# A two-layer hybrid trunk: gated retention output turned by DMA, the gate's projection finished by token halves, weights requested in another order

## The chip, the cores and the metric

One core of a Trainium2 chip runs the whole kernel. The metric is the device time of one execution in microseconds (us). A core has five engines with a queue of instructions each: TensorE (PE; PEld is its weight load), VectorE (DVE), ScalarE (ACT), GpSimd (POOL) and SyncE (SP). An engine works through its queue in order, and an instruction that waits holds all that stand behind it. SyncE issues nearly all transfers (DMA).

## The reference, cut to what matters

Two layers run over x of 256 tokens by 1024. In each, one projection makes eight groups of 512 columns, RQ RK RV RZ for the retention heads and MQ MK MV MZ for the attention heads; the two gated outputs go side by side through w_out; then a gated embedding is added. The part that the change touches is the retention output and its gate:

```python
h = rms_norm(x, norm_g[i])
proj = h @ w_in[i]
rq, rk, rv, rz, mq, mk, mv, mz = jnp.split(proj, cuts, axis=-1)
r_out = retention(rotary(heads(rq, RET_HEADS), pos), rotary(heads(rk, RET_HEADS), pos),
                  heads(rv, RET_HEADS), ret_norm_g[i])
r_out = jax.nn.silu(rz.astype(f32)) * r_out
...
y = jnp.concatenate([r_out, m_out], axis=-1).astype(x.dtype) @ w_out[i]
x = x + y
gate = jax.nn.sigmoid((rms_norm(x) @ w_ple_gate[i]).astype(f32))
e = rms_norm(p[i] @ w_ple[i], ple_norm_g[i]).astype(f32)
x = x + (gate * e).astype(x.dtype)
```

All is float32. The retention output is normalised per head and multiplied by the gain ret_norm_g.

## The kernel before

The tokens stand in two halves of 128 (m = 0, 1). Every large product is done with three TensorE matmuls (`mm3`, L136): weights and activations are split into a high part (wh, ah: a cast to fp32r) and a low part (wl, al: the rest), and hi x hi, hi x lo and lo x hi are summed in PSUM.

A block of weights is 512 rows by 512 columns, 1 MB; each group of 512 columns needs two, half 0 and half 1 of the 1024 rows. The list `jobs` holds their loads in the order of use. `fetch` (L102) issues loads from SyncE until the wanted one is there and more than AHEAD = 3 loaded ones are unused. `load_w` (L123) fetches a block and splits it in two pieces, with a cast on ScalarE (L131) and a subtraction on VectorE (L132) each. Four blocks fit in the buffers wst, six pieces in wh and six in wl.

The order per layer is MQ, MK, MV, MZ, RQ, RK, RV, RZ, then w_out, then the gate of the embedding. TensorE's and SyncE's queues keep the order of the program. For ScalarE, VectorE and GpSimd a scheduler sets the order when the kernel is built. Work that belongs between the matmuls is put there by `later(n, f)`: it runs f after n ticks, and a tick comes after every six matmuls of `project`.

`project` (L379) makes the groups MQ, MK, MV, RV and RZ with tokens on the partitions: for each block, four k by two m, k outermost; m is outermost only in the second block of MQ in layer 1 (L387). `project_turned` (L437) makes RQ and RK with the head's columns on the partitions, and for each head `rope` (L479) reads the accumulator: ScalarE copies one half of it (L486), VectorE adds the other (L487), which frees it. There are four accumulators, so head 2 of RK needs the one of head 2 of RQ. `moba_scores` (L518), its `turn` and `moba_out` (L561, whose matmuls have lines L566 and L567) are the attention's steps that lie between these.

q and k of the attention are turned from tokens to columns by DMA: `qk_norm` (L416) makes the rows, `halves` (L396) splits each float into two 16-bit halves on ScalarE (L399), and 6 + m ticks later `to_heads` (L402) issues a 16-bit DMA transpose from SyncE (L407) and puts the halves together again with two VectorE copies (L412). SyncE also writes the row scales out (`spread`) and reads them back over all partitions (`gather`, hrow), and loads the constants cst, which rope reads.

The retention output is turned on TensorE. `ret_out` (L590) leaves the normalised rows in RO. `gate` (L500) makes silu's factor of RZ from a tanh (L504) and L505. `ret_gate` (L611) multiplies both (L613); 4 + m ticks later its `turn` does four 128x128 transposes on TensorE into PSUM (L242), and `evac_parts` (L244) multiplies by the gain (L250), casts the high part (L253) and subtracts for the low part (L254). The result yT[m], blocks 0 to 3, is read by the last part of w_out: first both column halves n of the attention's rows of w_out (half 1, 48 matmuls), then those of the retention's rows (half 0) for m = 0 and for m = 1. After that come the embedding's product and the gate's.

## Time and profile before

| what | us |
|---|---|
| median of 3 runs | 320.6 (320.49 to 322.58) |
| profiled execution, its own time | 321.39 |
| span of the profiled execution | 319.5 |
| TensorE busy in the span | 311.8 |
| VectorE busy | 240.0 |
| ScalarE busy | 197.5 |
| GpSimd busy | 27.4 |

The profile is of one execution. Its span runs from the first to the last instruction of the core; the execution's own time also has what lies around it. Times in the trace count from the start of the span. Matmuls are pipelined: a row's duration is longer than the distance to the next one. An idle time in brackets is that of the engine just before the instruction, with what ended it.

### The profile page before, as it was taken

The page shows a single profiled execution, that of the slowest core. Times are in us where ns is not written, and L with a number is a line of the kernel's source. Part 1 is how long each engine was busy: PE and PEld are TensorE (multiplying, and loading weights), DVE is VectorE, ACT ScalarE, POOL GpSimd, SP SyncE. Part 2 cuts the span into 40 slices and gives each one's busy share as a digit, 9 for nine tenths or more (in the row PEclk, how much of TensorE's full clock was granted, in tenths as well). Part 3 has the DMA queues.
Part 4 walks back from the last instruction along what each step waited for, and adds up shares of the span by engine and source line. Part 5 has one row for each costly group of instructions (what it writes and reads, how often), then busy time and mean ns, then how long its engine had stood idle before and what let it go on. Part 6 is the DMA issues. An engine that isn't in the chain of part 4 may idle for free.

```text
span 319.5 us, 4520 instructions
## 1 busy us (share of the span) xinstructions
PE 311.8 (98%) x1625; PEld 264.8 (83%) x1625; DVE 240.0 (75%) x436; ACT 197.5 (62%) x378; POOL 27.4 (9%) x45
## 2 busy tenths in 40 slices
PE   8999999979999999999999999999999999999994
PEld 4888899868888888888888888998888888888884
DVE  4797856979967985958798877586799669859632
ACT  5878836986943544836485987559769424438411
POOL 4014200000001100011001521000000011000000
PEclk9999999999999999999999999999999999999999
DMA  7996999742673365000997169973345533610001
GB/s 272 416 401 210 284 291 416 263 147 118 228 267 132 131 242 188 0 2 4 373 409 255 78 151 247 389 286 131 131 144 201 184 133 131 220 44 2 33 33 68
DMA packets 19126, 61.13 MB, mean 191 GB/s; under 512 B 9628, under 2 KB 10656, under 8 KB 12960
## 3 DMA queue, kind: packets, MB, share of 16 engines
q1 hardware_dynamic: 19096, 60.85, 54.5%
q8 instruction: 13, 0.21, 0.3%
q14 instruction: 9, 0.07, 0.1%
q10 hardware_dynamic: 8, 0.00, 0.0%
HBM read 57.69 MB, written 1.06 MB: 184 GB/s over the span
## 4 chain that ended last, share of the span: by engine, by line
PE 74%; DMA 9%; ACT 8%; DVE 4%; issue 2%; SPq 1%; ACTq 0%
PE acc L139 17%; PE acc L141 17%; PE acc L140 17%; DMA wst<-in_w_in 6%; PE acc L449 6%; ACT wh L131 3%; PE acc L450 3%; PE mix L242 2%; PE mix L557 2%; DMA E<-in_rest 2%; DVE wl L132 2%; DMA w<-u 2%; PE acc L472 1%; PE acc L470 1%; PE acc L468 1%
## 5 line engine op out<-in xcount | busy, mean ns | idle before, releaser
L132 DVE TENSOR_TENSOR wl<-wst,wh 128x1024 fp32r<-128x1024 f32 x96 | 115.8, 1221 | 26.8 <-ACT wh L131 26.6
L131 ACT CAST wh<-wst 128x1024 fp32r<-128x1024 f32 x96 | 98.5, 1051 | 59.5 <-PE acc L141 30.4
L139 PE MATMUL acc<-wh,a 128*128 128x512 f32 (+1 forms) x296 | 116.4, 393 | 0.0
L140 PE MATMUL acc<-wl,a 128*128 128x512 f32 (+1 forms) x296 | 113.8, 385 | 0.1
L141 PE MATMUL acc<-wh,a 128*128 128x512 f32 (+1 forms) x296 | 113.8, 384 | 0.0
L141 PEld LDWEIGHTS acc<-wh,a 128*128 128x128 f32 x296 | 55.6, 188 | 11.2
L139 PEld LDWEIGHTS acc<-wh,a 128*128 128x128 f32 x296 | 55.8, 189 | 10.7 <-ACT wh L229 0.6
L140 PEld LDWEIGHTS acc<-wl,a 128*128 128x128 f32 x296 | 55.8, 189 | 10.6 <-DVE wl L236 0.6
L449 PE MATMUL acc<-a,wh 128*128 128x512 f32 x128 | 46.6, 406 | 2.0 <-DVE tmp L487 2.0
L450 PE MATMUL acc<-a,wl 128*128 128x256 f32 x128 | 35.8, 280 | 0.0
L449 PEld LDWEIGHTS acc<-a,wh 128*128 128x128 f32 x128 | 24.1, 188 | 7.6 <-issue 1.9
L450 PEld LDWEIGHTS acc<-a,wl 128*128 128x128 f32 x128 | 24.2, 189 | 0.1
L468 PE MATMUL acc<-a,wh 128*128 128x256 f32 x64 | 18.6, 291 | 0.0
L472 PE MATMUL acc<-a,wl 128*128 128x256 f32 x64 | 18.1, 283 | 0.0
L470 PE MATMUL acc<-a,wh 128*128 128x256 f32 x64 | 18.1, 283 | 0.0
L712 ACT ACTIVATE tmp<-acc,hr 128x512 f32<-128x512 f32 (+1 forms) x9 | 5.8, 640 | 19.4 <-PE acc L141 17.7
L152 POOL TENSOR_TENSOR ro<-rs_t,neghalf 128x4 f32<-128x4 f32 x4 | 4.0, 1007 | 142.7 <-DVE rs_t L151 142.7
L713 DVE SCALAR_TENSOR_TENSOR tmp<-tmp,E 128x512 f32<-128x512 f32 (+1 forms) x9 | 5.7, 631 | 13.7 <-ACT tmp L712 13.7
L412 DVE COPY T<-w 128x512 uint16<-128x512 uint16 x16 | 6.4, 459 | 9.0 <-DMA w<-u 9.0
L468 PEld LDWEIGHTS acc<-a,wh 128*128 128x128 f32 x64 | 12.3, 192 | 0.1
L470 PEld LDWEIGHTS acc<-a,wh 128*128 128x128 f32 x64 | 12.3, 192 | 0.1
L472 PEld LDWEIGHTS acc<-a,wl 128*128 128x128 f32 x64 | 12.2, 191 | 0.0
(119 smaller groups left out, 376.4 us busy)
## 6 DMA issues: line engine op xcount, KB each, us to landing
wst<-in_w_in SPq DMA_DIRECT2D x30, 1024.0 KB, 8.4
wst<-in_w_out SPq DMA_DIRECT2D x8, 1024.0 KB, 4.7
wst<-in_w_gate SPq DMA_DIRECT2D x8, 1024.0 KB, 4.8
wst<-in_w_ple SPq DMA_DIRECT2D x2, 1024.0 KB, 4.7
wst<-in_rest SPq DMA_DIRECT2D x4, 384.0 KB, 6.6
E<-in_rest SPq DMA_DIRECT2D x3, 384.0 KB, 4.0
x_t<-in_x SPq DMA_DIRECT2D x2, 512.0 KB
gb<-in_ple_g SPq DMA_DIRECT2D x2, 512.0 KB, 4.4
```

The lines of the kernel that those rows point to most:

```text
L131: nc.scalar.copy(hi, s)
L132: nc.vector.tensor_tensor(lo, s, hi.bitcast(F32), op=ALU.subtract)
L139: nc.tensor.matmul(ps, ah[:, k], wh[:, kk], start=start, stop=False)
L140: nc.tensor.matmul(ps, ah[:, k], wl[:, kk], start=False, stop=False)
L141: nc.tensor.matmul(ps, al[:, k], wh[:, kk], start=False, stop=stop)
L242: nc.tensor.transpose(ps[:, j * P:(j + 1) * P], src[:, b * P:(b + 1) * P], ident)
L412: nc.vector.tensor_copy(raw[:, t], w[:, t])
L449: nc.tensor.matmul(ps[h], wh[:, k % 2, sl], aB[:, kk], start=kk == 0, stop=False)
L450: nc.tensor.matmul(ps[h][:, 0], wl[:, k % 2, sl], aB[:, kk, 0], start=False, stop=end)
L468: nc.tensor.matmul(o, wh[:, k % 2, sl], aB[:, kk, 0], start=kk == 0 and h % 2 == 0, stop=False, skip_group_check=True)
L470: nc.tensor.matmul(o, wh[:, k % 2, sl], aB[:, kk, 1], start=False, stop=False, skip_group_check=True)
L472: nc.tensor.matmul(o, wl[:, k % 2, sl], aB[:, kk, 0], start=False, stop=end, skip_group_check=True)
```

## The change

The four parts of the change:

- `ret_gate` no longer turns its product on TensorE. It splits it into 16-bit halves (`halves`, moved out and shared), and 1 + 2m ticks later `parts_by_dma` issues a DMA transpose from SyncE, puts the halves together with two VectorE copies into a tile in SBUF and gives that to `evac_parts`.
- The second block of RZ is done for m = 0 first and then for m = 1.
- `fetch` no longer loads ahead. `ahead` does so at the end of `load_w` and `load_first`, after the block's split has been put into the program, and when the block counts as used; so one block more is requested there than before.
- The constants are requested after the second block of RQ instead of after the first, the transposes of q and k come at tick 7 + m instead of 6 + m, and `spread` at 8 instead of 9.

```diff
     def fetch(key):
 
-        while key not in got or len(got) - len(used) <= AHEAD:
-            if not jobs:
-                break
-            k, fn = jobs.pop(0)
-            r = fn()
-            if k is not None:
-                got[k] = r
+        while key not in got:
+            load_next()
         used.add(key)
         return got[key]
+
+    def load_next():
+        k, fn = jobs.pop(0)
+        r = fn()
+        if k is not None:
+            got[k] = r
+
+    def ahead():
+
+        while jobs and len(got) - len(used) <= AHEAD:
+            load_next()
...
             parts.append((hi, lo))
+        ahead()
         return parts
...
+    def turned_by_dma(u, raw):
+
+
+        w = tok_p.tile([P, 2, 4, P], U16, name="w16", bufs=2)
+        nc.sync.dma_start(w.rearrange("p t h k -> p (t h) k"), u.rearrange("p t n -> p (t n)"),
+                          transpose=True)
+        for t in range(2):
+            nc.vector.tensor_copy(raw[:, t], w[:, t])
+
+    def parts_by_dma(a, k0, u, gains=None):
+
+        with tc.high_priority(offset=PRIO):
+            f = tmp_p.tile([P, GW], F32, name="tmp")
+            turned_by_dma(u, f.bitcast(U16).rearrange("p (j k t) -> p t j k", j=4, t=2))
+            evac_parts(a, k0, f, 4, gains)
...
-                if l == 0 and g == RQ and not half:
+                if l == 0 and g == RQ and half:
                     job(None, lambda: nc.sync.dma_start(cst, consts))
...
-                if half and l and g == MQ:
+                if half and (g == RZ or l and g == MQ):
                     rows.sort(key=lambda r: r[1])
...
-                later(6 + m, lambda m=m, u=u: to_heads(g, m, u, qkg[:, l:l + 1] if g == MQ else None))
+                later(7 + m, lambda m=m, u=u: to_heads(g, m, u, qkg[:, l:l + 1] if g == MQ else None))
...
             nc.vector.tensor_tensor(y, RO[m], G[RZ][:, m], op=ALU.mult)
 
-            def turn():
-                pt = mix_p.tile([P, 512], F32, name="mix")
-                transposed(y, range(H), pt)
-                evac_parts(yT[m], 0, pt, H, par[:, Q_RG + l * H:Q_RG + (l + 1) * H])
-            later(4 + m, turn)
+            u = halves(y)
+            later(1 + 2 * m, lambda: parts_by_dma(yT[m], 0, u, par[:, Q_RG + l * H:Q_RG + (l + 1) * H]))
...
-        later(9, spread)
+        later(8, spread)
```

SyncE's queue in layer 0, around the requests for RQ's weights. Before, from the second block of MZ on (w_385 and w_438 are the transposes of MQ, w_484 and w_495 those of MK, hd the row scales written out, hrow these read back, cst the constants; the request after the transpose of MQ's second half is RQ's first block, and the first of the seven at the end its second):

```order
L119 DMA wst<-in_w_in 128x2048
L371 DMA hd_141<-hrt 4x32 x2
L407 DMA_TRANSPOSE w_438<-u_335 128x8x128
L119 DMA wst<-in_w_in 128x2048
L407 DMA_TRANSPOSE w_484<-u_402 128x8x128
L375 DMA hrow<-hd_141 128x256
L407 DMA_TRANSPOSE w_495<-u_416 128x8x128
L317 DMA cst<-in_consts 128x1536
L119 DMA wst<-in_w_in 128x2048 x7
```

And now, from both blocks of MZ on (w_435 and w_446 of MQ, w_493 and w_503 of MK):

```order
L125 DMA wst<-in_w_in 128x2048 x2
L401 DMA hd_141<-hrt 4x32 x2
L125 DMA wst<-in_w_in 128x2048
L262 DMA_TRANSPOSE w_435<-u_324 128x8x128
L262 DMA_TRANSPOSE w_446<-u_338 128x8x128
L125 DMA wst<-in_w_in 128x2048
L405 DMA hrow<-hd_141 128x256
L262 DMA_TRANSPOSE w_493<-u_400 128x8x128
L262 DMA_TRANSPOSE w_503<-u_414 128x8x128
L347 DMA cst<-in_consts 128x1536
L125 DMA wst<-in_w_in 128x2048 x6
```

Both blocks of RQ now stand ahead of the transposes of MK, and the second one ahead of the constants.

ScalarE's queue in layer 0 where RQ's second block ends and RK begins, from the copy for rope of RQ's head 0 on. Before:

```order
L486 COPY tmp<-acc 128x256
L548 COPY PS<-mix 128x4x128
L541 ACTIVATE tok<-tok,ri 128x256 x2
L486 COPY tmp<-acc 128x256
L488 COPY tmp<-tmp 64x256
L489 COPY tmp<-tmp 64x256
L548 COPY PS<-mix 128x2x256
L131 CAST wh<-wst 128x1024
L488 COPY tmp<-tmp 64x256
L489 COPY tmp<-tmp 64x256
L131 CAST wh<-wst 128x1024
```

And now, from the same copy on:

```order
L506 COPY tmp<-acc 128x256
L568 COPY PS<-mix 128x4x128
L506 COPY tmp<-acc 128x256
L568 COPY PS<-mix 128x2x256
L508 COPY tmp<-tmp 64x256
L509 COPY tmp<-tmp 64x256
L508 COPY tmp<-tmp 64x256
L509 COPY tmp<-tmp 64x256
L137 CAST wh<-wst 128x1024 x2
L568 COPY PS<-mix 128x2x256
L506 COPY tmp<-acc 128x256 x2
```

The softmax's division (L541) has moved ahead of this stretch, and the two copies for rope stand together. In layer 1 the kernel before has the rows of the second piece already, with its own line numbers.

VectorE's queue in layer 0 from the gate of RZ to the retention output's split. Before (G is the gate, tok its product with the output, mix the turned product in PSUM, par the gain):

```order
L505 SCALAR_TENSOR_TENSOR G<-tmp,acc 128x512 x2
L132 TENSOR_TENSOR wl<-wst,wh 128x1024
L613 TENSOR_TENSOR tok<-T,G 128x512 x2
L132 TENSOR_TENSOR wl<-wst,wh 128x1024
L250 TENSOR_TENSOR tmp<-mix,par 128x512
L132 TENSOR_TENSOR wl<-wst,wh 128x1024
L254 TENSOR_TENSOR a<-tmp,a 128x4x128
L250 TENSOR_TENSOR tmp<-mix,par 128x512
```

And now (w_1230 is the transposed product of m = 0, u16 halves):

```order
L525 SCALAR_TENSOR_TENSOR G<-tmp,acc 128x512
L633 TENSOR_TENSOR tok<-T,G 128x512
L621 TENSOR_SCALAR ro_1152<-ro,rstd_309 128x4
L138 TENSOR_TENSOR wl<-wst,wh 128x1024
L627 TENSOR_SCALAR T<-mix,bmv,ro_1152 128x128 x4
L525 SCALAR_TENSOR_TENSOR G<-tmp,acc 128x512
L138 TENSOR_TENSOR wl<-wst,wh 128x1024
L265 COPY tmp<-w_1230 128x512 x2
L633 TENSOR_TENSOR tok<-T,G 128x512
L138 TENSOR_TENSOR wl<-wst,wh 128x1024
L280 TENSOR_TENSOR tmp<-tmp,par 128x512
L138 TENSOR_TENSOR wl<-wst,wh 128x1024
```

The gate and the product of m = 0 have moved ahead of the normalisation of m = 1, and the two copies of the turned m = 0 stand ahead of the product of m = 1.

## Rows read from the trace of the kernel before

**Rows 1.** Busy times of the engines over the span, from the page.
```profile
PE 311.8 (98%) x1625; PEld 264.8 (83%) x1625; DVE 240.0 (75%) x436; ACT 197.5 (62%) x378; POOL 27.4 (9%) x45
```

**Rows 2.** TensorE's waits: line, releaser, us in total, times, longest.
```profile
PE acc L449 <- DVE tmp L487: 2.0, 2, 1.7
```

**Rows 3.** TensorE's timeline, RK's head 2 in layers 0 and 1: start, us, instruction.
```profile
71.25 0.47 PE L449 MATMUL acc<-a,wh 128*128 128x512 f32 x1 [1.72 <-DVE tmp L487]
...
231.34 0.47 PE L449 MATMUL acc<-a,wh 128*128 128x512 f32 x1 [0.29 <-DVE tmp L487]
```

**Rows 4.** TensorE's timeline around the first group of transposes of tok.
```profile
113.39 0.39 PE L141 MATMUL acc<-wh,a 128*128 128x512 f32 x1
113.62 0.60 PE L242 MATMUL mix<-ident,tok 128*128 128x128 f32 x4
113.98 0.48 PE L139 MATMUL acc<-wh,a 128*128 128x512 f32 x1
114.29 0.40 PE L140 MATMUL acc<-wl,a 128*128 128x512 f32 x1
```

**Rows 5.** SyncE's timeline: requests and transposes.
```profile
34.75 1.25 SPq L407 DMA_TRANSPOSE w<-u  x1
...
42.74 0.42 SPq L119 DMA_DIRECT2D wst<-in_w_in  x1
...
257.12 19.47 SPq L119 DMA_DIRECT2D wst<-in_w_gate  x4
```

**Rows 6.** ScalarE's timeline: casts of RQ's second block (both layers) and of RV's first.
```profile
50.20 1.05 ACT L131 CAST wh<-wst 128x1024 fp32r<-128x1024 f32 x1 [6.23 <-DMA wst<-in_w_in]
...
205.18 1.05 ACT L131 CAST wh<-wst 128x1024 fp32r<-128x1024 f32 x1 [3.27 <-PE acc L470]
...
227.42 1.05 ACT L131 CAST wh<-wst 128x1024 fp32r<-128x1024 f32 x1
```

**Rows 7.** VectorE's timeline: the copy of MK's first transpose, L487 for RQ's head 2.
```profile
43.08 0.47 DVE L412 COPY T<-w 128x512 uint16<-128x512 uint16 x1 [3.13 <-DMA w<-u]
...
70.68 0.42 DVE L487 TENSOR_TENSOR tmp<-acc,tmp 128x256 f32<-128x256 f32 x1
...
230.77 0.42 DVE L487 TENSOR_TENSOR tmp<-acc,tmp 128x256 f32<-128x256 f32 x1
```

**Rows 8.** Instruction groups by shape: count, busy us, mean ns, idle before.
```profile
L132 DVE TENSOR_TENSOR wl<-wst,wh 128x1024 fp32r<-128x1024 f32 x96 | 115.8, 1221 | 26.8 <-ACT wh L131 26.6
L131 ACT CAST wh<-wst 128x1024 fp32r<-128x1024 f32 x96 | 98.5, 1051 | 59.5 <-PE acc L141 30.4 <-DMA wst<-in_w_in 13.6 <-DVE T L607 7.0
L399 ACT COPY u<-tok 128x1024 uint16<-128x1024 uint16 x8 | 8.5, 1058 | 0.3 <-DVE tok L431 0.3
L412 DVE COPY T<-w 128x512 uint16<-128x512 uint16 x16 | 6.4, 459 | 9.0 <-DMA w<-u 9.0
L250 DVE TENSOR_TENSOR tmp<-mix,par 128x512 f32<-128x512 f32 x8 | 5.5, 687 | 0.2
L253 ACT CAST a<-tmp 128x512 fp32r<-128x512 f32 x8 | 5.0, 620 | 2.0 <-DVE tmp L250 1.8
```

**Rows 9.** TensorE's timeline: first scores, RZ's second block, w_out's last part for m=0, m=1.
```profile
47.08 1.05 PE L526 MATMUL mix<-T 128*128 128x128 f32 x8
...
102.64 0.48 PE L139 MATMUL acc<-wh,a 128*128 128x512 f32 x1
...
120.00 0.39 PE L139 MATMUL acc<-wh,a 128*128 128x512 f32 x1
...
125.80 0.48 PE L139 MATMUL acc<-wh,a 128*128 128x512 f32 x1
```

**Rows 10.** The transposes of all 8 issues (tile w), from issue to landing.
```profile
DMA to landing us min/median/max: 3.1/3.9/5.3
```

**Rows 11.** DMA issues by line: KB each, median us from issue to landing.
```profile
wst<-in_w_ple SPq DMA_DIRECT2D x2, 1024.0 KB, 4.7
```

**Rows 12.** TensorE's timeline: the embedding's first matmul in layer 0.
```profile
131.84 0.39 PE L139 MATMUL mix<-wh,ph 128*128 128x512 f32 x1
```

More of the change, by code (lines that the diff above doesn't have):

```diff
@@ L237, in load_first @@
             parts.append((hi, lo))
+        ahead()
         return parts
@@ L242, in transposed, with halves @@
             nc.tensor.transpose(ps[:, j * P:(j + 1) * P], src[:, b * P:(b + 1) * P], ident)
+    def halves(src):
+        u = tok_p.tile([P, 2, GW], U16, name="u16", bufs=3)
+        nc.scalar.copy(u, src.bitcast(U16).rearrange("p (n t) -> p t n", t=2))
+        return u
+    def turned_by_dma(u, raw):
[9 more added lines that the diff above has]
+            evac_parts(a, k0, f, 4, gains)
     def evac_parts(a, k0, ps, n, gains=None):
@@ L394, in project @@
             return ps
-        def halves(src):
-            u = tok_p.tile([P, 2, GW], U16, name="u16", bufs=3)
-            nc.scalar.copy(u, src.bitcast(U16).rearrange("p (n t) -> p t n", t=2))
-            return u
         def to_heads(name, m, u, scale=None):
@@ L405, in to_heads @@
                 T[name] = big.tile([P, H, S], F32, name="T")
-            w = tok_p.tile([P, 2, H, P], U16, name="w16", bufs=2)
-            nc.sync.dma_start(w.rearrange("p t h k -> p (t h) k"), u.rearrange("p t n -> p (t n)"),
-                              transpose=True)
             dst = T[name][:, :, m * P:(m + 1) * P]
             raw = T[name].bitcast(U16).rearrange("p h (k t) -> p t h k", t=2)[:, :, :, m * P:(m + 1) * P]
-            for t in range(2):
-                nc.vector.tensor_copy(raw[:, t], w[:, t])
+            turned_by_dma(u, raw)
             if scale is not None:
```

## Prediction, made before the changed kernel was run

> **What bounds the kernel now.** I read first the busy times, then who made TensorE wait, then TensorE's own instructions in order of time. TensorE is busy for 311.8 of 319.5 us [rows 1], and the reader is to see in the list of its waits that only one line held it in a layer's work: two waits, 2.0 us together, for VectorE's L487 [rows 2]. The timeline shows one in each layer, at the matmul with which RK's head 2 begins: 1.72 us before 71.25 and 0.29 before 231.34 [rows 3]. (A matmul of 512 columns takes 0.39, its successor starts after 0.227, as at 113.39 and 113.62 [rows 4], so each wait costs TensorE up to 0.17 more than its row says: 1.89 and 0.46.) All other time is matmul after matmul. So two things shorten this kernel: fewer TensorE instructions, or less of those two waits. What happens on the other engines costs nothing until it makes TensorE wait anew.
>
> **The wait in layer 0.** RK's head 2 needs the accumulator that rope of RQ's head 2 frees with L487. L487 stands late by a chain that starts at SyncE: the second half of RQ's weights is requested only at 42.74 [rows 5], behind the transposes of MK and the constants; ScalarE, idle for 6.23 us, converts it at 50.20 [rows 6], 21.1 us before 71.25; the softmax work of this stretch is pressed together behind that, and L487 runs at 70.68 [rows 7]. The change requests that half ahead of those transposes and the constants, once a buffer is free (MV's second half split) and MQ's two transposes are issued; the transpose before which it now stands was issued at 34.75 [rows 5], so I put the request there at the latest, and the landing 7.5 us later, as from 42.74 to 50.20, at 42. The conversion then waits for its own buffers, which MZ's first half holds on TensorE, not for the transfer. So it is in layer 1, where TensorE's L470 releases it at 205.18 [rows 6], 26.2 us before 231.34. ScalarE's order in layer 0 becomes row for row that of layer 1 before, and TensorE's order around it is the same in both. So I take layer 1's wait as the value: 1.72 becomes 0.29, a gain of 1.43. What is late next is the same L487: at 230.77 [rows 7] it stands, by the order, behind two subtractions fed by conversions from 227.42 [rows 6]. That order is unchanged, so I leave 0.29 standing in both layers. Bounds: none of layer 0's wait goes (0), or both go whole (1.89 + 0.46 = 2.35).
>
> **Transposes taken off TensorE.** Four groups of four go, two a layer. The matmul before a group starts at 113.39, the next L139 at 113.98: 0.59 where 0.227 is usual; that L139 is followed at 114.29, 0.31 later [rows 4]. A group costs 0.36 + 0.085 = 0.445, four cost 1.78. All of it is on the path, if the turned data come in time.
>
> **What the turned half now costs, and what covers it.** Per half of the tokens it adds a ScalarE split (1.06), a DMA transpose and two VectorE copies (0.46 each); multiply (0.69), cast (0.62) and subtract (as the multiply) remain [rows 8]. The question is the deadline. I put it on the clock of before. RZ's second half starts at 102.64 [rows 9]. Done by tokens, m=0 is finished after 12 of 24 matmuls, at 102.64 + 0.08 + 11 x 0.227 + 0.39 = 105.6. Tanh, gate and product at some 0.7 each (as the multiply) end at 107.7. ScalarE first converts a weight whose buffer RZ now holds until its 18th matmul, 107.0 (by the same count); that takes 1.05 [rows 8], and the split ends at 109.1. SyncE issues the transpose then, and it lands L later. Transposes took 3.1 to 5.3 us, median 3.9 [rows 10]; no weight should be in flight before these, so 3.1 is near, but I take 3.9.
> VectorE waits at the two copies, and behind them in its queue stand the product of m=1, a weight's subtraction (1.22) and the multiply. The high part of m=0 is ready at 109.1 + L + 0.92 + 0.69 + 1.22 + 0.69 + 0.62 = 113.2 + L, or 117.1; the low part, behind one more subtraction, at 114.5 + L = 118.4. TensorE asks for them at 120.00 [rows 9] less the two groups taken away, 119.1, and for the low part 0.45 later: 2.0 and 1.1 us to spare. They fail from L = 5.0. For m=1 the split stands behind a conversion that waits for the matmul at 113.39 [rows 4], so it ends at 113.39 + 0.39 + 1.05 + 1.06 = 115.9; landing 119.8, ready 122.0 and 122.7; asked for at 125.80 [rows 9] less 0.9, 124.9. So nothing is added to the path at the median; at 5.3 the low part is 0.3 late, 0.6 for both layers, which have the same order and distances.
>
> The Trainium skill ("VectorE: DVE Perf Modes", section "The three transpose paths" and the rules below it) speaks against this edit: it advises TensorE for a 128x128 transpose where a PSUM destination will do, at 390 ns against 1309 ns by DMA. Eight 16-bit blocks at its figure would be an estimate of 10.5 us a half, far past the deadline. The trace does not agree: eight such blocks landed within 5.3 us [rows 10].
>
> **Order on SyncE.** In layer 0 the transposes stand ahead of the embedding's and the gate's weights (in layer 1 one of the gate's goes ahead). They hold those until 115.9 + 1.25 [rows 5] = 117.2. The embedding's weights land 4.7 us after a request [rows 11], at 121.9; with a conversion and a subtraction 124.2, and TensorE asks at 131.84 [rows 12] less 0.9. Hidden, with over 6 us; the gate's are asked for later still. Requests made one step sooner elsewhere wait for the same buffers as before: nothing, as TensorE waited for no weight. The transposes of q and k are a tick later in the program: nothing, since MK's first was copied at 43.08 [rows 7], MK's transfers have the same work ahead of them, and the scores follow at 47.08 [rows 9]; 4 us cover it. Rows sorted by m: no instruction more.
>
> **The sum.** 319.5 - 1.43 - 1.78 = 316.3 us of span. The profiled execution took 321.39, 1.9 outside its span; the median of the runs is 320.6, so 1.1 over that span: 317.4.
>
> **Rivals.**
> Both waits go (chance 0.17). For: earlier conversions take load off ScalarE. Against: the order before L487 in layer 1 is unchanged. 319.5 - 1.78 - 2.35 + 1.1 = 316.5.
> The transposes go but layer 0's wait stays (0.14), if L487 is held by the two subtractions and not by the late weights; against it stands layer 1. 320.6 - 1.78 = 318.8.
> The turned half is a little late (0.11), L = 5.9. Past L = 5.7 a layer loses 2L - 10.7: m=0's lateness, L - 5.0, and the rest from m=1, whose product waits in VectorE's queue for m=0's transfer. That is 1.1 a layer, 2.3 with rounding in all: 319.7.
> Slower (0.06): a transpose queues behind weights in flight. For: one issued at 34.75 [rows 5], close behind a weight request, let VectorE go on at 43.08 [rows 7], 8.3 us. At L = 8.3 a layer loses 5.9, so 317.4 + 11.9 = 329.3; it is slower by 1% from L = 6.9. Against: the last weight request ahead of the transposes is long landed: in layer 1 it is the gate's first, at 257.12 [rows 5], and the layers lie 160.1 apart (71.25 to 231.34), so the split ends at 269.2, 12 us later.
>
> **How the numbers follow.** The forecast has 0.52, with a range of its own of 316.9 to 317.9. A measurement of this kernel tells about 1% from no change, 3.2 us, so the line is 317.4 and cuts the forecast in two. Faster by over 1%: 0.26 + 0.17 = 0.43. Within 1%: 0.26 + 0.14 + 0.11 = 0.51. Slower: 0.06. The range for 8 in 10 runs from just under the first rival, 316.2, past the third, 320.4; it leaves out the slow case and the edges.
>
> **What would show it.** Right: no transposes of tok between the parts of w_out, their neighbours 0.227 apart; 0.3 us of wait at RK's head 2 in both layers; the conversions of RQ's second half released by TensorE and not by a transfer; the turned half's copies over before 116 and 122 on the old clock. Wrong: TensorE waiting at the first matmul of either token half of w_out's last part, for a cast or a subtraction; a wait for a weight; RK's head 2 still held for 1.7 us.

## The result, and the profile of the changed kernel

| | before, in the same comparison | after |
|---|---|---|
| median, us | 321.59 (320.49 to 322.58, 4 runs) | 318.35 (317.61 to 318.54, 4 runs) |
| ratio to before | 1 | 0.9888, 95% interval 0.9859 to 0.9918 |
| profiled execution: time, span | 321.39, 319.5 | 318.17, 316.0 |

The changed kernel is 1.1% faster. The profiled span fell by 3.5 us, where the prediction's sum had 3.2.

The page's busy times and TensorE's list of waits (line, releaser, us in total, times, longest) answer to [rows 1, 2]. L507 is the old L487, L469 the old L449:

```profile
PE 310.0 (98%) x1609; PEld 263.2 (83%) x1609; DVE 243.3 (77%) x444; ACT 201.0 (64%) x382; POOL 27.5 (9%) x45
...
PE acc L469 <- DVE tmp L507: 0.6, 2, 0.3
```

TensorE has 16 instructions less, the four groups of four transposes, and is busy for 1.8 us less. Of the two waits for rope's addition the one of 1.7 us has become one of 0.3. TensorE's timeline at RK's head 2 in layers 0 and 1, then between the two column halves of w_out's first part and at the first matmul for m = 0 and for m = 1 of its last part, answers to [rows 3, 4, 9]:

```profile
69.54 0.47 PE L469 MATMUL acc<-a,wh 128*128 128x512 f32 x1 [0.29 <-DVE tmp L507]
...
111.85 0.39 PE L148 MATMUL acc<-wh,a 128*128 128x512 f32 x1
112.08 0.39 PE L146 MATMUL acc<-wh,a 128*128 128x512 f32 x1
...
117.52 0.39 PE L146 MATMUL acc<-wh,a 128*128 128x512 f32 x1
...
123.32 0.48 PE L146 MATMUL acc<-wh,a 128*128 128x512 f32 x1
...
228.86 0.47 PE L469 MATMUL acc<-a,wh 128*128 128x512 f32 x1 [0.31 <-DVE tmp L507]
```

From 111.85 to 112.08 it is 0.23, the usual distance: no group of transposes stands there any more. No row of w_out's last part has a wait in brackets, so the turned half comes in time. SyncE's, ScalarE's and VectorE's timelines show how (start, us, instruction, idle before it and what ended it). SyncE first, around RQ's second block (at 35.21) and around the turned output:

```profile
28.45 6.66 SPq L262 DMA_TRANSPOSE w<-u  x2
35.21 0.53 SPq L125 DMA_DIRECT2D wst<-in_w_in  x1
...
38.91 3.04 SPq L262 DMA_TRANSPOSE w<-u  x2
42.00 0.57 SPq L347 DMA_DIRECT2D cst<-in_consts  x1
...
107.50 8.37 SPq L262 DMA_TRANSPOSE w<-u  x2
115.96 0.52 SPq L125 DMA_DIRECT2D wst<-in_w_ple  x1
```

ScalarE: the cast of RQ's second block, then the split of the gated product (L255) and the high parts (L283) for m = 0 and m = 1:

```profile
43.38 2.00 ACT L137 CAST wh<-wst 128x1024 fp32r<-128x1024 f32 x2 [1.97 <-PE acc L490]
...
106.44 1.04 ACT L255 COPY u<-tok 128x1024 uint16<-128x1024 uint16 x1
...
113.57 1.04 ACT L255 COPY u<-tok 128x1024 uint16<-128x1024 uint16 x1
114.51 0.62 ACT L283 CAST a<-tmp 128x512 fp32r<-128x512 f32 x1
119.30 0.62 ACT L283 CAST a<-tmp 128x512 fp32r<-128x512 f32 x1 [4.17 <-DVE tmp L280]
```

VectorE: the copies that put the turned halves together (L265) and the low parts (L284):

```profile
110.71 0.79 DVE L265 COPY tmp<-w 128x512 uint16<-128x512 uint16 x2
...
115.16 0.69 DVE L284 TENSOR_TENSOR a<-tmp,a 128x512 fp32r<-128x512 f32 x1 [0.22 <-ACT a L283]
117.74 0.80 DVE L265 COPY tmp<-w 128x512 uint16<-128x512 uint16 x2 [1.89 <-DMA w<-u]
...
119.96 0.69 DVE L284 TENSOR_TENSOR a<-tmp,a 128x512 fp32r<-128x512 f32 x1 [0.69 <-ACT a L283]
```

The reader is to see two chains with room to spare. RQ's second block, asked for 7.5 us sooner than before, is there when its cast runs: the cast waits for TensorE, not for the transfer, as layer 1's did in [rows 6]. And m = 0's parts are ready at 115.1 and 115.9 (L283 and L284 and their durations), while TensorE asks at 117.52 and, for the low part, at 117.97; m = 1's are ready at 119.9 and 120.7 against 123.32.

### The profile page after: what moved, and what is told of

It reads as the page before. It is cut to its first block, busy times and chain, and to the rows that moved or that the text cites. A ratio compares the mean times of both kernels' runs of the same rounds, so it can differ in the third digit from the quotient of the medians.

```text
span 316.0 us, 4502 instructions
## 1 busy us (share of the span) xinstructions
PE 310.0 (98%) x1609; PEld 263.2 (83%) x1609; DVE 243.3 (77%) x444; ACT 201.0 (64%) x382; POOL 27.5 (9%) x45
## 4 chain that ended last, share of the span: by engine, by line
PE 94%; ACT 2%; DVE 1%; issue 1%
PE acc L146 21%; PE acc L147 21%; PE acc L148 21%; PE acc L469 8%; PE acc L470 4%; PE acc L492 2%; PE acc L490 2%; PE acc L488 2%; PE mix L250 2%; PE mix L577 2%; PE mix L546 2%; PE mix L169 1%; PE mix L146 1%; PE mix L147 1%; PE mix L148 1%
## 5 line engine op out<-in xcount | busy, mean ns | idle before, releaser
L138 DVE TENSOR_TENSOR wl<-wst,wh 128x1024 fp32r<-128x1024 f32 x96 | 115.6, 1219 | 24.4 <-ACT wh L137 23.7
L146 PEld LDWEIGHTS acc<-wh,a 128*128 128x128 f32 x296 | 55.8, 188 | 10.7 <-ACT wh L236 0.4
L469 PE MATMUL acc<-a,wh 128*128 128x512 f32 x128 | 46.8, 407 | 0.6 <-DVE tmp L507 0.6
L469 PEld LDWEIGHTS acc<-a,wh 128*128 128x128 f32 x128 | 24.1, 188 | 6.3 <-PE mix L587 0.9
L490 PE MATMUL acc<-a,wh 128*128 128x256 f32 x64 | 18.1, 283 | 0.0
L730 DVE SCALAR_TENSOR_TENSOR tmp<-tmp,E 128x512 f32<-128x512 f32 (+1 forms) x9 | 5.7, 631 | 12.7 <-ACT tmp L729 12.7
L255 ACT COPY u<-tok 128x1024 uint16<-128x1024 uint16 x12 | 12.6, 1062 | 0.3 <-DVE tok L451 0.3
L490 PEld LDWEIGHTS acc<-a,wh 128*128 128x128 f32 x64 | 12.3, 192 | 0.1
```

Source lines behind the costliest of these rows:

```text
L138: nc.vector.tensor_tensor(lo, s, hi.bitcast(F32), op=ALU.subtract)
L146: nc.tensor.matmul(ps, ah[:, k], wh[:, kk], start=start, stop=False)
L255: nc.scalar.copy(u, src.bitcast(U16).rearrange("p (n t) -> p t n", t=2))
L469: nc.tensor.matmul(ps[h], wh[:, k % 2, sl], aB[:, kk], start=kk == 0, stop=False)
L490: nc.tensor.matmul(o, wh[:, k % 2, sl], aB[:, kk, 1], start=False, stop=False, skip_group_check=True)
```

## The experiments

The theory was the prediction's own: 1.43 us come from the sooner request of RQ's second block, 1.78 us from TensorE's transposes, and the turned half costs nothing while it is in time. The rivals were that it is one of the two alone, that another edit does it, and that the turned half has little room.

### One part at a time

e1_order_only makes only the edits of the order (`ahead`, the place of the constants, the ticks 7 + m and 8). Against the changed kernel it undoes the rest:

```diff
-            u = halves(y)
-            later(1 + 2 * m, lambda: parts_by_dma(yT[m], 0, u, ...))
+            def turn():
+                pt = mix_p.tile([P, 512], F32, name="mix")
+                transposed(y, range(H), pt)
+                evac_parts(yT[m], 0, pt, H, ...)
+            later(4 + m, turn)
...
-                if half and (g == RZ or l and g == MQ):
+                if half and l and g == MQ:
```

> The kernel before with only the requests in the new order (ahead, constants behind RQ's second block, the q and k transposes and spread one tick apart); the retention output is turned on TensorE as before. Theory (two gains that add up): the conversions of RQ's second half are released by TensorE near 43.5, the wait at RK's head 2 in layer 0 falls from 1.72 to 0.29, the four groups of transposes of tok stay. Span 319.5 - 1.43 = 318.1, ratio to before about 0.9955. Rival A (the requests do nothing by themselves, the whole gain is the transposes'): wait still 1.7, span 319.5, ratio 1.000. Rival B (all of the 3.5 us is the requests'): 316.0, ratio 0.989.

Measured: 320.38 us (319.79 to 321.14, 10 runs) against 321.81 for before in the same comparison, ratio 0.9962 (0.9948 to 0.9975), span 318.0. In TensorE's list of waits both are 0.3:

```profile
PE acc L457 <- DVE tmp L495: 0.6, 2, 0.3
```

So the order alone gives 1.5 us of span in the profiles and 0.4% of the time, 1.2 us (0.8 to 1.7).

e2_turn_only is the other part alone, with the requests, constants and ticks as before:

```diff
-        while key not in got:
-            load_next()
+        while key not in got or len(got) - len(used) <= AHEAD:
+            ...
...
-        ahead()
...
-                if l == 0 and g == RQ and half:
+                if l == 0 and g == RQ and not half:
-                later(7 + m, ...)
+                later(6 + m, ...)
...
-        later(8, spread)
+        later(9, spread)
```

> The kernel before with only the retention output turned by DMA and RZ's second block done by token halves; the requests, the constants and the ticks as before. Theory: the four groups go, 1.78 us; the wait at RK's head 2 in layer 0 stays at 1.7, in layer 1 at 0.3; no wait at w_out's last part. Span 319.5 - 1.8 = 317.7, ratio about 0.9945. Rival A (the transposes were hidden anyway, the gain is the requests'): 319.5. Rival B (without the sooner requests the transposes hold weights on SyncE and TensorE waits for them): over 318.5, with a wait of TensorE at the embedding or the gate.

Measured: 318.88 us (318.72 to 319.74, 4 runs), ratio 0.9916 (0.9894 to 0.9938), span 316.7. The gain is there, and is larger than expected: the interval ends at 0.9938, short of the 0.9945. In the profiled execution the wait in layer 0 was 0.3 where 1.7 was expected, in a stretch where the program is that of the kernel before. This was profiled again, and the kernel before too:

> The kernel with the turn alone (requests as before) profiled once more. Layer 0 up to w_out is there the same program as the kernel before, whose two profiles both waited 1.7 us at RK's head 2, while this one's first waited 0.3. Theory (the wait follows the time at which RQ's second block starts to be cast, and that varies with how long transposing instructions hold SyncE): cast at 47.9 again gives 0.3 and span 316.7, cast at 50 or later gives 1.7 and span 318.1. Rival (the new program is laid out so that the wait is gone for good): cast at 47 to 48, 0.3 again.

> The kernel before, unchanged, profiled a second time. Theory (the request order fixes layer 0's wait): TensorE's wait at RK's head 2 is 1.7 us again in layer 0 and 0.3 in layer 1, RQ's second block is requested at 42.7 and its first cast starts at 50.2, and the span is 319.5. Rival (the wait follows how long SyncE was held by the transposing instructions ahead of that request, and this varies from run to run of one program): the request comes at 41 to 43 and the wait at 0.3 to 1.7, the earlier the request the shorter the wait, with a span shorter by what the wait is (318.1 at 0.3).

Measured: e2 a second time has a span of 317.7 and the wait of 1.7 back; the kernel before has the 1.7 again, with a span of 320.6 (0.8 of the 1.1 us more have come up before RK's head 2 of layer 0, 0.3 of them another wait). SyncE's hold at MK's second transpose, ScalarE's cast of RQ's second block and TensorE at RK's head 2, first in e2, then in e2 once more; last the hold in the kernel before:

```profile
39.50 1.24 SPq L254 DMA_TRANSPOSE w<-u  x1
47.92 2.00 ACT L131 CAST wh<-wst 128x1024 fp32r<-128x1024 f32 x2 [4.78 <-DMA wst<-in_w_in]
...
70.19 0.47 PE L461 MATMUL acc<-a,wh 128*128 128x512 f32 x1 [0.28 <-DVE tmp L499]
```

```profile
39.26 2.46 SPq L254 DMA_TRANSPOSE w<-u  x1
50.28 2.00 ACT L131 CAST wh<-wst 128x1024 fp32r<-128x1024 f32 x2 [6.64 <-DMA wst<-in_w_in]
...
71.33 0.47 PE L461 MATMUL acc<-a,wh 128*128 128x512 f32 x1 [1.73 <-DVE tmp L499]
```

```profile
38.99 3.08 SPq L407 DMA_TRANSPOSE w<-u  x1
```

The same instruction held SyncE for 1.24 us in one run and 2.46 in the next, RQ's second block was requested behind it and the constants at 41.41 and 42.40, and the cast came at 47.92 or 50.28: a wait of 0.3 or of 1.7. So the later request is 1.0 of the 2.4 us between the casts; the other 1.4 lie between request and cast (6.5 and 7.9 us), and why is not shown. In the kernel before, the transpose held SyncE for 3.08 us (then 3.47), the cast came at 50.20 (51.04), and the wait was 1.7 both times. So the theory's cause holds, the late cast, but its size is a matter of the run where the request stands behind MK's transposes.

For the other term, the second run of e2 has the same waits as before and 319.5 - 317.7 = 1.8 us less span. One pair of executions is little where two of the kernel before lie 1.1 apart, so here is the part that doesn't hold layer 0's wait, from RK's head 2 of layer 0 to the end of the span:

| profiled execution | RK's head 2 starts, us | from there to the end, us |
|---|---|---|
| before, before again, e1 (turn on TensorE) | 71.25, 72.08, 69.44 | 248.2, 248.5, 248.6 |
| changed, e2, e2 again (turn by DMA) | 69.54, 70.19, 71.33 | 246.5, 246.5, 246.3 |

The turn by DMA gains 2.0 us there, 1.7 to 2.2 from pair to pair, whatever the wait ahead of it was.

### Which edit of the order does it

e5_old_fetch goes back to the old loop in `fetch`, and keeps the constants behind RQ's second block. e4_consts_first keeps the new loop and puts the constants back:

```diff
-        while key not in got:
+        while key not in got or len(got) - len(used) <= AHEAD:
...
-        ahead()
```

```diff
-                if l == 0 and g == RQ and half:
+                if l == 0 and g == RQ and not half:
```

> The changed kernel with the old loop that requests weights (one stage later, and before the casts instead of behind them); constants, ticks, the turn by DMA and the order of the gate's second half stay changed. Theory (the sooner request is the part that takes the wait away): RQ's second block goes out behind MK's two transposes, at 42 instead of 35.2, its casts again come late, and layer 0's wait at RK's head 2 is 1.4 to 1.7; span 317.4. Rival (a request at 42.0, ahead of the constants, is already soon enough, so that moving the constants alone does it): wait 0.3, span 316.0. The turned halves are in time in both; the four groups of transposes stay gone.

> The changed kernel with the constants' transfer back ahead of RQ's second block (0.6 us of SyncE and 768 KB in front of it); ScalarE's order in RQ's and RK's stages falls back to that of the kernel before. Theory (time of the request decides, not ScalarE's order): request at 35.8 to 36, still six us sooner than before, so the wait at RK's head 2 in layer 0 stays at 0.3; span 316.0. Rival (the order in which ScalarE does the rope's copies and the casts is what makes the wait): wait 1.4 to 1.7 again, span 317.4.

Measured: e5 318.16 us, span 316.1; e4 317.69, span 315.8 (one run each, with a profile). In both, layer 0's wait is gone and the 0.3 left is layer 1's. e5's transposes of MK, its request and cast, then e4's request and cast:

```profile
36.45 2.61 SPq L254 DMA_TRANSPOSE w<-u  x2
39.12 0.60 SPq L119 DMA_DIRECT2D wst<-in_w_in  x1
44.32 2.00 ACT L131 CAST wh<-wst 128x1024 fp32r<-128x1024 f32 x2 [2.65 <-DMA wst<-in_w_in]
```

```profile
35.77 0.37 SPq L125 DMA_DIRECT2D wst<-in_w_in  x1
43.76 2.00 ACT L137 CAST wh<-wst 128x1024 fp32r<-128x1024 f32 x2 [2.04 <-PE acc L490]
```

The theory missed for e5: it had the request at 42 and the wait at 1.4 to 1.7, but the request went out at 39.12 and the cast came at 44.3. The constants, which no longer stand in front, are only 0.6 us of that (42.12 to 42.74 in the kernel before). The other 3 are MK's transposes: SyncE is through with the second at 39.06, where it was at 42.07. It issues it 1.2 us sooner and is held by it for 1.3 us in place of 3.1, and the hold, as seen above, varies from run to run. e5 and e4 both keep the changed ticks of the transposes and of `spread`, which put the reading of hrow ahead of both of MK's transposes. So with these ticks either of the two edits was enough, in one run each; the ticks by themselves, and each edit with the old ticks, were not run. For e4 the theory held, against the rival that ScalarE's order makes the wait of 1.7. It had 0.3 left in layer 0, though, and none was: in e4 ScalarE's copies and casts there are back in nearly the order of before, so the 0.3 in the changed kernel may come with its new order, which was not tested by itself. The transfer needs to be little sooner, not the 7 us that the change gives it: in e2's first run 1.3 were enough.

### The sort of RZ's rows

```diff
-                if half and (g == RZ or l and g == MQ):
+                if half and l and g == MQ:
```

> The changed kernel with RZ's second block in the old order (k outermost), all else kept. Theory (the deadline of the turned half, by the sum of durations): the product of m=0 comes some 4 us later, the split ends near 112 and the transpose lands near 115; the high part of m=0 is ready near 117.2 and the low part near 118.6, asked for at 117.5 and 118.0. So TensorE waits some 0.6 us a layer at w_out's last part: span 316.0 + 1.3 = 317.3 (0.3 to 1.5 a layer). Rival (the deadline is loose, the sort is worth nothing): 316.0 and no wait there.

Measured: 324.85 us (323.66 to 326.4, 4 runs), ratio 1.0099 (1.0062 to 1.0136), slower than before. The profiled execution is the longest of the four, 326.4, with a span of 324.3. The expectation, 1.3 us over the changed kernel, was far too low. TensorE's list of waits, two of its rows where the clock falls and rises again, and a table of layer 1 by stretches (us, then busy time and instructions of PE, PEld, DVE, ACT, POOL, then the granted clock of TensorE, the share of the DMA engines and GB/s):

```profile
PE acc L148 <- DVE a L284: 2.2, 2, 1.2
PE acc L146 <- ACT a L283: 1.7, 1, 1.7
...
282.54 0.80 PE L148 MATMUL acc<-wh,a 128*128 128x512 f32 x1 [1.21 <-DVE a L284]
...
288.67 0.39 PE L147 MATMUL acc<-wl,a 128*128 128x512 f32 x1
...
275.00:280.00 5.00, 3.89 (x18) 2.88 (x16) 4.56 (x7) 2.16 (x4) 0.00 (x0) 1.00 1.00 269
280.00:285.00 5.00, 3.19 (x8) 2.28 (x9) 3.12 (x4) 1.17 (x3) 0.00 (x0) 0.68 1.01 426
285.00:290.00 5.00, 5.00 (x16) 3.93 (x15) 0.69 (x1) 0.72 (x2) 0.00 (x0) 0.64 0.04 15
```

Without the sort both token halves of RZ end together, the turn starts later, and TensorE waits 3.9 us in both layers together for the parts of w_out's last part. Layer 0's 0.96 is within the 0.3 to 1.5 expected, layer 1's 2.9 is not. The copies begin as late in both (14.3 and 14.1 us after RZ's second block starts), but in layer 1 VectorE has two weight subtractions and ScalarE a cast between these and the parts: the low part ends 6.1 us after the copies begin, in layer 0 3.9. So about 2 us are the scheduler's order and not lateness. In layer 1's waits TensorE was busy for 3.89 and 3.19 of 5.00 us, and the granted clock of the second of these stretches and of the next is 0.68 and 0.64: the two levels of 2.4 and 1.2 GHz mixed. From 282.54 to 288.67 fourteen matmuls take 6.1 us where they take 14 x 0.227 = 3.2 at the full clock: another 2.9. Together 6.8 of the 8.3 us over the changed kernel's span; the rest I didn't trace. The clock doesn't make the verdict: one of the four runs had a mean granted clock of 1.000 and took 323.66, still over the longest of the 13 runs of before beside it, 322.43. The sort, which adds no instruction and was priced at nothing, is what makes the turn by DMA pay.

### How late a turned half may come

These put a transfer of the split halves to DRAM, used by nothing, right ahead of m = 0's transposing DMA in each layer, of 2 MB and of 1 MB (4 in place of 8).

```diff
+                if m == 0:
+                    bulk = dram.tile([P, 8, 2 * GW], U16, name=f"bulk{l}")
+                    nc.sync.dma_start(bulk, u...[:, None, :].to_broadcast([P, 8, 2 * GW]))
                 parts_by_dma(yT[m], 0, u, ...)
```

> The changed kernel with a DMA of 2 MB (a transfer of the same halves to DRAM, eight times over, used by nothing) right ahead of the transpose of m=0 in each layer: the rival that a turned half comes late because its DMA lies behind bytes in flight. Theory: the 2 MB take about 5 us of the 16 engines (1 MB of weights alone lands in some 3 to 4.6), the first half then lands about 5 us later, its lo part at about 121 against 118.0 where TensorE asks; the second half has less delay. TensorE waits 1.5 to 3 us at the first group of w_out's last part in each layer, span 319.5 (318.5 to 322). Rival (the transpose goes beside the bulk and is not held up): no such wait, span 316.0 to 316.5.

> The same transfer ahead of m=0's transpose with 1 MB in place of 2. Theory (a transposing DMA lands 3.1 us after its issue with nothing ahead, and later by what the bytes ahead of it take): 3.1 alone and 9.8 behind 2 MB give 6.4 behind 1 MB (a transpose behind 1 MB of weights took 7.1 elsewhere). The first half's parts are then 3.4 to 4 us later than in the changed kernel, where they had 2.4 and 2.1 us to spare: TensorE waits 1 to 2 us a layer at w_out's last part, span 318 to 320, and such short waits leave the clock at full speed. Rival (the delay comes with any transfer ahead, whatever its size): landing near 9.8, waits of 3.5 us a layer and a lower clock behind them, span 328.

Measured, by one profiled run each: with 2 MB 330.6 us, span 328.7; with 1 MB 319.34, span 317.4. The landing of layer 0's transposes (first both of the changed kernel, then with 1 MB and with 2 MB that of m = 0 alone, as the trace has none for m = 1) and TensorE's timeline at w_out's last part; for 2 MB also its waits over both layers and two stretches of layer 0, with the columns of the table above:

```profile
DMA to landing us min/median/max: 3.1/3.1/3.1
```

```profile
DMA to landing us min/median/max: 6.8/6.8/6.8
...
119.09 0.50 PE L148 MATMUL acc<-wh,a 128*128 128x512 f32 x1 [0.15 <-DVE a L284]
```

```profile
DMA to landing us min/median/max: 9.8/9.8/9.8
...
PE acc L146 <- ACT a L283: 4.7, 2, 2.6
PE acc L148 <- DVE a L284: 2.3, 2, 1.6
...
120.11 0.50 PE L146 MATMUL acc<-wh,a 128*128 128x512 f32 x1 [2.56 <-ACT a L283]
...
121.48 0.79 PE L148 MATMUL acc<-wh,a 128*128 128x512 f32 x1 [0.64 <-DVE a L284]
...
127.61 0.39 PE L147 MATMUL acc<-wl,a 128*128 128x512 f32 x1
...
120.00:125.00 5.00, 4.25 (x10) 3.10 (x11) 4.45 (x6) 2.57 (x4) 0.00 (x0) 0.57 1.01 421
125.00:130.00 5.00, 5.00 (x20) 3.97 (x19) 1.04 (x2) 0.72 (x2) 0.00 (x0) 0.74 1.01 419
```

The landing follows the bytes ahead: 3.1, 6.8 and 9.8 us for m = 0 in layer 0, and 3.0, 5.5 and 8.4 in layer 1. What that does to TensorE is far from even. At 6.8 it waits 0.15 us in layer 0 and at 5.5 not at all in layer 1, where m = 1's transpose landed in 3.1. So the 1 to 2 us a layer expected were too much: in this build the scheduler lets VectorE do m = 1's product and one more weight subtraction ahead of the copies, and so the parts follow the copies sooner (the copies start at 115.77 and the low part ends 3.3 us later, where the changed kernel took 5.1). Of the 1.4 us over the changed kernel's span 0.9 have come up before the first scores, far ahead of the edit. With 2 MB it waits 7.0 us in both layers together, above the 3 to 6 expected, and the granted clock falls behind the wait, to 0.57 and 0.74 in these stretches of layer 0 and less in layer 1 (0.80 and 0.86): by the same count of matmuls 2.9 us (121.48 to 127.61) and 1.7. These make 11.6 of the 12.7 us over the changed kernel. The expectation, a span of 318.5 to 322, had no place for the clock.

### Versions that might beat both

e7_rope_in_place adds to the changed kernel that rope's copy goes into its own result, so that a head takes one tmp buffer less:

```diff
-            b = tmp_p.tile([P, S], F32, name="tmp")
+            b = dst
```

> The changed kernel with one edit: rope copies the second half of the accumulator into its result tile in place of a second temporary, so the four temporaries serve four heads and not two. Theory (the 0.29 us that is left at RK's head 2 in both layers comes from head 2's copies waiting for head 0's temporaries, and the order then puts two weight subtractions ahead of L507): both waits go, with the 0.17 each that a wait costs besides: span 316.0 - 0.9 = 315.1, ratio to before 0.986. Rival (the wait is VectorE's load and not the temporaries): wait still 0.3, span 316.0; or another wait appears in RQ and RK, as the order of ScalarE and VectorE changes there.

Measured: 317.35 us (317.11 to 318.05, 4 runs), ratio 0.9866 (0.9845 to 0.9888), span 315.4, and no wait for L507 in either layer. Whether the buffer or the new order that it gives the scheduler does it was not separated. It is the fastest kernel of this study, though its interval overlaps that of the changed kernel.

e8_moba_turn and e9_moba_turn_later carry the turn by DMA to the probabilities, on top of e7: tick 5 and tick 9 for the transposing DMA.

```diff
+                us.append(halves(s))
...
-                transposed(s, range(4), pt)
-                nc.scalar.copy(PT[...], pt...)
-            later(8, turn)
+                nc.sync.dma_start(w..., us[0]..., transpose=True)
+                for t in range(2):
+                    nc.vector.tensor_copy(raw[:, t], w[:, t]...)
+            later(5, turn)
```

> The changed kernel with the rope's copy in place, and in it the other turn of tok, the probabilities' (three groups of four 128x128 blocks a layer on TensorE), done by DMA as well: ScalarE splits the divided probabilities, a transposing DMA turns them, VectorE copies them into place. Theory (what the turn by DMA gains is TensorE's time for the transposes, as long as the turned half is in time): six groups go, 6 x 0.445 = 2.7 us, span 312.7 against 315.4 of the kernel with the copy in place; the halves are ready at 58 to 62 and asked for at 68.5, so a landing of up to 6 us is hidden. Rival (here the transposes lie behind weights in flight: 4 MB are requested between 42 and 62): landing 8 to 12 us, VectorE, which has the copies in its order ahead of weight subtractions and rope, stands waiting, and TensorE waits 2 to 6 us a layer in RQ, RK or the first outputs: span 317 to 325.

> The probabilities' turn by DMA again, with its transposing DMAs later in SyncE's order: behind the request of RQ's second... RK's first weights that they held up in the run before it (there SyncE stood at a transpose from about 47 until its data was ready at 60.2, and a request that could go at 47 went out at 65), two of them ahead of the next request, the third behind it. Theory (that run lost because a waiting transpose held requests behind it, not because a transpose is dear): weights go out at 47 and 57 again, the halves land at 61 to 69, and the turn's 2.7 us are won as far as the last half (ready at 63, asked for at 71) is in time: span 312.7, up to 315.5 with a wait of 1 to 1.4 us a layer at the first outputs. Rival (a transposing DMA among weights in flight lands late wherever it stands): waits of 2 us and more a layer again at the first outputs, span 317 to 321.

Measured: e8 ratio 1.0017 (0.999 to 1.0044); e9 322.11 us, ratio 1.0025 (0.9986 to 1.0063): 2.7 us were to be won and some 5 were lost against e7. The rivals' waits came in both, 4.9 and 4.5 us over the two layers; the landings of 8 to 12 us that e8's rival gave did not (two copies began some 3 us after the issue, the third 7.6). From e9's profiled execution, which took 323.92 with a span of 322.0, SyncE's queue and layer 0's wait:

```profile
59.33 1.24 SPq L569 DMA_TRANSPOSE w<-u  x1
...
64.31 0.53 SPq L125 DMA_DIRECT2D wst<-in_w_in  x1
65.00 1.28 SPq L569 DMA_TRANSPOSE w<-u  x1
...
72.15 0.79 DVE L573 COPY PS<-w 128x512 uint16<-128x512 uint16 x2 [0.40 <-DMA w<-u]
72.99 0.70 PE L591 MATMUL mix<-PS,V 128*128 128x256 f32 x2 [2.51 <-DVE PS L573]
```

The two halves issued ahead of the weights landed in 3.1 us. The third stands 0.7 us behind a request of 1 MB and its copy starts 7.2 us after its issue, as late as the 1 MB in the experiment above would have it, but here the first outputs ask for it at 70.5. The transposes also held back the weights: a request that e7 sends at 56.61 left at 64.31, where the theory had 57; in e8 the one of 47.35 left at 65.12. Of the 9.3 us between this execution and the 312.7 of the theory, waits for the probabilities are 4.5; of the rest, a part lies in smaller waits and, in layer 1, in a granted clock of 0.66 from 235 to 240, behind a wait of 2.0; I didn't add it up.

## Why the prediction was right, and where it was off

**What bounds the kernel**: right. The span fell by what TensorE lost in instructions and waits, though VectorE and ScalarE were busier by 3.3 and 3.5 us.

**Layer 0's wait, 1.43**: right in mechanism and size (1.5 of span in e1's profile, 1.2 in its timed runs). Request by 34.75 at the latest: 35.21, half a us past that, with room to spare. Cast released by TensorE's L490 in place of the transfer, as forecast. The step gave the sooner request and the constants as one cause; e4 and e5 show that either is enough with the new ticks. It gave the ticks no effect, but in e5 most of the time by which the request is sooner lies in MK's transposes, which the ticks move. What the step did not see either is that the wait before is not a constant of the program: e2's first profile, of the same order, had 0.3. That the wait was 1.7 in the one profile the prediction had, and so its price nearly the whole of 1.43, is in part luck.

**Four groups, 1.78**: 1.8 by the busy time, 2.0 (1.7 to 2.2) by the six profiles compared behind RK's head 2.

**The turned half**: the distances were right on a clock that runs 1.54 us earlier (RZ's second block starts at 101.10 where it was 102.64). Split of m = 0 over at 109.1 - 1.5 = 107.6: measured 107.5. Parts of m = 0 at 115.6 and 116.9 with L = 3.9: measured 115.1 and 115.9 with L = 3.1, the value that the prediction named as near and did not take. Split of m = 1 over at 114.4: measured 114.6; parts at 120.5 and 121.2: measured 119.9 and 120.7. "They fail from L = 5.0" fits the changed kernel: its low part has 2.1 us to spare at L = 3.1, so it fails from 5.2. e6_bulk_1mb bore 6.8 with a wait of 0.15, but in another order: there the scheduler places m = 1's product and a weight's subtraction ahead of the copies, so 1.8 us less lie between these and the low part. The limit belongs to VectorE's order. As for L, [rows 10] have landings for only five of the eight transposes; the one issued at 34.75 has none, and its copy could start only 8.3 us later, as the prediction's last rival says.

**Order on SyncE**: right. The embedding's weights were requested at 115.96, where 117.2 on the old clock is 115.7, and TensorE waited for no weight behind them.

**Rows sorted by m**: "no instruction more" is true, but its worth lies in the deadline and in the order that the scheduler makes around it: without it the changed kernel (e3) was slower than before by 1%.

**The last step, from span to time**: here the number was off by 1.0. The sum gave a span of 316.3, and the four timed runs have 315.7, 316.0, 316.5 and 316.5. But 1.1 us was then added, the median of the runs shown less the span of the profiled one, which mixes two executions. What lies outside the span is 1.9 to 2.2 us in each run of after, and 1.9 in the profiled one of before. With 2.0 the sum is 318.3, and 318.35 was measured. That lies outside the forecast's own range, 316.9 to 317.9, and inside the wide one only because that has room for the rivals. As a ratio the forecast was 317.4 / 320.6 = 0.990 against 0.9888 (0.9859 to 0.9918): before's median too came out 1.0 higher in the comparison, 321.59, so the two errors cancel there. Faster by over 1%, as the median has it, had been given 0.43; the interval holds both sides of the line.

**The rivals**: the wait did not stay, and no half was late. Both waits gone takes one more edit, and its price holds: a span of 315.4 in e7, where 319.5 - 1.78 - 2.35 = 315.4. The slower case is real where bytes lie ahead of the transposes, but its price was made up wrongly. For L = 9.8 and 8.4, as in e6_bulk_2mb's two layers, 2L - 10.7 gives 8.9 + 6.1 = 15.0 us, all of it lateness. 12.7 were lost: 7.0 in waits, all of them for m = 0's parts, and 4.6 by the clock, which the price left out. m = 1's share did not come, as VectorE does m = 1's product ahead of the copies in that build too.

The Trainium skill ("VectorE: DVE Perf Modes", "The three transpose paths") would make the eight blocks of a half about 10.5 us at its 1309 ns each, an estimate. The trace doesn't agree: it had 3.0 to 3.1 us for the three halves of the turned output whose landing it has (of four), with nothing in flight. The same page of the Trainium skill ("Rules for kernel authors") advises TensorE where a PSUM destination will do. That did not hold for this turn, which gained, and did for that of e8 and e9, which lost.

## What to carry to other kernels

A transpose can be taken off a bound TensorE and given to DMA, at a gain of just the matmuls that go, if three things are read off the trace first: when the data is ready, when it is asked for, and what lies in the DMA queues in between. Make the producer finish by halves, so that the first turn starts early; issue the transposing DMA ahead of the next weight requests, but only where it doesn't hold them until they are needed. A wait that ends with a transfer may come and go from run to run, so profile a second time before you price its removal.

## What was not expected of the hardware

The landing of the same eight 16-bit blocks went from 3.0 us with nothing in flight to 6.8 behind 1 MB and 9.8 behind 2 MB, and up to 6.7 among weights in layer 0's attention of the changed kernel. The hold of one transposing instruction on SyncE varied from 1.24 to 2.46 us between two runs of one program. And waits of 1.7 to 2.6 us on TensorE in the middle of a layer had two outcomes. At RK's head 2 of the kernel before (1.7) and at the first outputs in e9's layer 0 (2.5) the granted clock stayed at 1.00. At the same first outputs in e9's layer 1 (2.0) it fell to 0.66 over the next five us, and at w_out's last part, in e3's layer 1 and e6_bulk_2mb's layer 0, fourteen matmuls ran at about half the rate, which cost 2.9 us each time, about as much again as the waits there (2.9 and 3.2). What tells the two outcomes apart is not shown.
